# One decoder layer on Trainium2: the MLP's two products as seven products of half-size blocks, in two stages with the combinations of u in DRAM

## The chip, the cores and the metric

The kernel runs on one core of a Trainium2 chip. The time is device microseconds of one execution; for the kernel before it is the median of 3 runs, 2079.65 us (2079.5 to 2080.16). Five engines of the core appear in the profile: PE (TensorE, the matrix products), DVE (VectorE), ACT (ScalarE), POOL (GpSimd) and SP, whose queue issues all the large DMA transfers here. PSUM is the memory that PE adds up into, in banks of 128 x 512 fp32; SBUF holds tiles of 128 partitions; DRAM is the chip's HBM.

## The reference, cut to what matters

One layer of a decoder with three mixers side by side, all in fp32; sequence 1024, width 1024, MLP width 4096.

```python
for l in range(DEPTH):                      # DEPTH = 1
    h = rms_norm(x, norm_mix_g[l])
    z_a, z_bx, z_by, z_q, z_k, z_v, z_g = split_cols(h @ w_in[l], IN_SIZES)
    ...                                     # three mixers, their projections, their gates
    merged = gates[:, :, 0] * y_a + gates[:, :, 1] * y_b + gates[:, :, 2] * y_c
    x = x + merged @ w_out[l]                        # 1024 x 1024 x 1024
    u = rms_norm(x, norm_mlp_g[l]) @ mlp_up[l]       # 1024 x 1024 x 4096
    x = x + jnp.square(jax.nn.relu(u)) @ mlp_down[l] # 1024 x 4096 x 1024
```

The change touches the last three lines alone.

## The kernel before

Every fp32 product of a 128 x 128 block with 512 columns is made of three matmuls: each operand is split in a rounded part "hi" and the rest "lo", and `mm3` adds hi·hi, hi·lo and lo·hi into one PSUM bank. `load_w` brings 512 KB of a weight from DRAM, casts hi on ACT (L225) and makes lo on POOL as raw − hi (L226); its rings hold 2 raw and 3 split blocks. PSUM has 8 banks, drawn from rings with the tags "g", "s" and "w" of two banks each and two single ones, "ac0" and "ac1".

`tail` is the end of the layer. It has these parts.

- **w_out.** For 4 groups of 256 columns two weight blocks are loaded, and for each of the 8 row tiles one bank takes 24 matmuls of 256 columns; DVE adds it to x2, which stays in SBUF (L1273). With the last column group each row tile is normalised (`norm_tile`, L254 to L256) into xn.
- **norm_split.** xn is transposed on PE, four 128 x 128 blocks to a bank (L264); ACT writes the scaled hi into hh (L266), DVE the lo into hl (L267). hh and hl hold the transposed, normalised x in two halves of 512 rows of the sequence. The first half is done among the w_out matmuls, the second half (`second_half`) after them.
- **up(f)**, 32 times. A block of 128 columns of mlp_up against both halves: 2 banks of 24 matmuls each. `ev` takes u out of the bank: relu and its square as hi on ACT (L1301, L1302), the square again on DVE in fp32 (L1303), lo on POOL (L1304). u stays in SBUF, in rings of 4.
- **down(c)**, 16 times, after the up blocks of the next chunk. Two 128-row blocks of mlp_down are loaded and split (ACT L1316, POOL L1317), and for each of 8 row tiles and 2 column halves a bank takes 6 matmuls; DVE adds each bank to x2 (L1325). With the last chunk each row tile is stored to the output (L1327).

The order of instructions on each engine is not written out by hand. The program is written in the order of the loops, and the framework's scheduler places each engine's instructions at build time by its own model of when they are ready; the semaphores then follow from the tiles that are read and written. A tile whose ring is full waits for the last reader of the tile that it replaces.

Of the kernel before, what the change touches and what calls it, by code (L numbers as in the profile page):

```python
# [18 lines left out]
P = 128  # L19
# [105 lines left out]
def hybrid_block(ctx, tc, io, out, dbg=None):  # L125
# [103 lines left out]
    def mm3(ps, pairs, first=True, last=True):  # L229

        n = len(pairs)
        for i, (lh, ll, rh, rl) in enumerate(pairs):
            PE.matmul(ps, lh, rh, start=first and i == 0, stop=False)  # L233
            PE.matmul(ps, lh, rl, start=False, stop=False)  # L234
            PE.matmul(ps, ll, rh, start=False, stop=last and i == n - 1)  # L235
# [1016 lines left out]
def tail(tc, io, last, dbg, psum, pg, mh_pool, mhi, mlo, load_w, mm3, gemm_pieces, norm_tile, norm_split, out):  # L1252
    nc = tc.nc
    V, A, G, S = nc.vector, nc.scalar, nc.gpsimd, nc.sync
    x2d, outd = io["x"][0], out[0]
    with tc.tile_pool(name="x2", bufs=1) as xp:
        x2 = xp.tile([P, 8, D], F32, name="x2")
        with tc.issue_after(last.ins):
            for i in range(8):
                S.dma_start(x2[:, i, :], x2d[i * P : (i + 1) * P, :])  # L1260
        hh, hl = ([xp.tile([P, KT, H], F32R, name=f"{nm}0")] for nm in ("hh2", "hl2"))
        n2 = tc.tile_pool(name="n2", bufs=2)
        np2 = n2.__enter__()
        xns = {}
        for n in range(4):
            cs = slice(n * 256, n * 256 + 256)
            wt = [load_w(io["w_out"][0][512 * q : 512 * q + 512, cs].rearrange("(k p) c -> p k c", p=P), [P, 4, 256], f"wo{n}{q}")
                  for q in range(2)]
            for i in range(8):
                ps = psum("s", 2, f"wo{n}{i}") if i % 2 else pg.tile([P, 512], F32, tag="g", name=f"wo{n}{i}")  # L1270
                hf, ts_ = i // 4, slice(i % 4 * P, (i % 4 + 1) * P)
# [10 lines left out]
        with tc.tile_pool(name="h2", bufs=1, side="right") as h2:  # L1282
# [8 lines left out]
            with tc.tile_pool(name="wd", bufs=1) as wd, tc.tile_pool(name="mu", bufs=2) as mu:  # L1291
# [38 lines left out]
                for c in range(nchunk + 1):  # L1330
# [3 lines left out]
                    if c > 0:  # L1334
                        down(c - 1)
# [24 lines left out]
```

## Time and profile before

| | |
|---|---|
| time, median of 3 runs | 2079.65 us (2079.5 to 2080.16) |
| time of the profiled execution | 2078.28 us |
| its span, first to last instruction | 2076.5 us |
| mean granted TensorE clock | 0.988 |
| all before w_out | about 1265 us of the span |
| w_out with the first half of the norm | about 1265 to 1360 us |
| second half of the norm, first up blocks | about 1360 to 1400 us |
| up and down blocks in turn | to 2072 us |
| w_out matmuls of 256 columns | 768 |
| MLP matmuls of 512 columns | 3072 |

The busy times of the profile are sums over instructions of an engine; PE and PEld are matmuls and the weight loads that run beside them. Matmuls overlap in the records: each of 512 columns shows about 390 ns, but they follow one another more closely, so the time of a stage is read from how many of them fall into a window and not from their durations. "idle before, releaser" gives what ended an engine's idle time. PEclk is the clock that PE was granted, 1.0 being full speed.

### The profile page before, as it was taken

What the parts mean: (1) busy time and instruction counts of PE and PEld (TensorE: products, weight loads), DVE (VectorE), ACT (ScalarE), POOL (GpSimd) and SP (SyncE); (2) the same over time, 40 slices, a digit from 0 to 9 for tenths busy, and PEclk for the clock granted to TensorE, in tenths of its full rate; (3) what the DMA queues carried; (4) which work ended last, traced back from release to release, by engine and by line L of the source; (5) the groups of instructions that cost most, each with busy time, mean ns of one, the idle gap of its engine ahead of it and who ended that gap; (6) DMA issues with size and microseconds to landing.
All of it is one profiled execution on the core that took longest, in us unless ns stands there. A gap on an engine that the chain in (4) does not pass through costs nothing. (4 is left out here: it accounts for less than half of the span.)

```text
span 2076.5 us, 30629 instructions
## 1 busy us (share of the span) xinstructions
PE 2012.3 (97%) x12486; PEld 1616.5 (78%) x12486; DVE 954.5 (46%) x1830; ACT 632.1 (30%) x1117; POOL 667.4 (32%) x606
## 2 busy tenths in 40 slices
PE   6999999999999999999999999999999999999999
PEld 4766777787778778677777789978888888888887
DVE  5665456556656653332342443163344443434434
ACT  5665223323332322332333222152221122211210
POOL 2223442344243331211543422135332233322320
PEclk9999999999999999999999999999999999999999
DMA  4222311222122214432543334122111111111102
GB/s 140 58 68 72 90 54 46 55 74 57 48 53 68 55 53 150 127 114 92 168 123 100 117 105 148 52 62 81 51 51 41 41 53 59 44 49 41 39 13 82
DMA packets 191907, 155.32 MB, mean 75 GB/s; under 512 B 36264, under 2 KB 167493, under 8 KB 191766
## 3 DMA queue, kind: packets, MB, share of 16 engines
q1 hardware_dynamic: 191590, 153.34, 24.6%
q8 instruction: 98, 1.61, 0.3%
q14 instruction: 43, 0.35, 0.1%
q0 software_dynamic: 160, 0.02, 0.0%
q10 hardware_dynamic: 16, 0.00, 0.0%
HBM read 125.15 MB, written 30.55 MB: 75 GB/s over the span
## 5 line engine op out<-in xcount | busy, mean ns | idle before, releaser
L1325 DVE TENSOR_TENSOR x<-dn,x 128x512 f32<-128x512 f32 x256 | 174.6, 689 | 256.4 <-PE dn L235 256.2
L233 PE MATMUL g_up<-hh,wh_up 128*128 128x512 f32 x512 | 199.8, 391 | 1.4 <-ACT r L1301 1.4
L234 PE MATMUL g_up<-hl,wh_up 128*128 128x512 f32 x512 | 200.7, 392 | 0.2 <-DVE hl L267 0.2
L235 PE MATMUL g_up<-hh,wl_up 128*128 128x512 f32 x512 | 199.6, 390 | 0.0
L233 PE MATMUL dn<-dh,uh 128*128 128x512 f32 x512 | 199.2, 389 | 0.0
L234 PE MATMUL dn<-dl,uh 128*128 128x512 f32 x512 | 199.2, 389 | 0.0
L235 PE MATMUL dn<-dh,ul 128*128 128x512 f32 x512 | 199.2, 389 | 0.0
L1303 DVE TENSOR_TENSOR r<-r 128x512 f32<-128x512 f32 x64 | 106.3, 1662 | 147.9 <-ACT uh L1302 147.9
L1317 POOL TENSOR_TENSOR dl<-dr,dh 128x1024 fp32r<-128x1024 f32 x32 | 76.7, 2419 | 285.0 <-ACT dh L1316 285.0
L233 PE MATMUL g_zg<-hh,wh_zg 128*128 128x512 f32 x384 | 155.5, 405 | 0.0
L234 PE MATMUL g_zg<-hl,wh_zg 128*128 128x512 f32 x384 | 152.8, 398 | 0.0
L235 PE MATMUL g_zg<-hh,wl_zg 128*128 128x512 f32 x384 | 152.6, 397 | 0.0
L1316 ACT CAST dh<-dr 128x1024 fp32r<-128x1024 f32 x32 | 32.3, 1052 | 318.0 <-PE dn L235 314.3
L233 PEld LDWEIGHTS g_up<-hh,wh_up 128*128 128x128 f32 x512 | 96.3, 188 | 21.8 <-ACT r L1301 1.9
L234 PEld LDWEIGHTS g_up<-hl,wh_up 128*128 128x128 f32 x512 | 96.3, 188 | 20.0 <-DVE hl L267 0.7
L234 PEld LDWEIGHTS dn<-dl,uh 128*128 128x128 f32 x512 | 96.2, 188 | 20.0
L235 PEld LDWEIGHTS dn<-dh,ul 128*128 128x128 f32 x512 | 96.1, 188 | 19.9
L233 PEld LDWEIGHTS dn<-dh,uh 128*128 128x128 f32 x512 | 96.1, 188 | 19.8
L235 PEld LDWEIGHTS g_up<-hh,wl_up 128*128 128x128 f32 x512 | 96.3, 188 | 19.4
L1304 POOL TENSOR_TENSOR ul<-r,uh 128x512 fp32r<-128x512 f32 x64 | 83.8, 1310 | 85.3 <-DVE r L1303 85.3
L226 POOL TENSOR_TENSOR wl_zg<-wr_zg,wh_zg 128x1024 fp32r<-128x1024 f32 x24 | 58.7, 2448 | 163.1 <-ACT wh_zg L225 145.3
L226 POOL TENSOR_TENSOR wl_up<-wr_up,wh_up 128x1024 fp32r<-128x1024 f32 x32 | 76.8, 2401 | 84.8 <-ACT wh_up L225 44.4
(435 smaller groups left out, 4622.8 us busy)
## 6 DMA issues: line engine op xcount, KB each, us to landing
wr_up<-in_mlp_up_dram SPq DMA_DIRECT2D x32, 512.0 KB
dr<-in_mlp_down_dram SPq DMA_DIRECT2D x32, 512.0 KB
wr_zg<-in_w_in_dram SPq DMA_DIRECT2D x24, 512.0 KB
mg_d<-th SPq DMA_DIRECT2D x32, 256.0 KB
tb<-mg_d SPq DMA_DIRECT2D x32, 256.0 KB
wr_z<-in_w_in_dram SPq DMA_DIRECT2D x12, 512.0 KB
qk_d<-zo SPq DMA_DIRECT2D x24, 256.0 KB
z<-qk_d SPq DMA_DIRECT2D x12, 512.0 KB
```

What stands on the lines that cost most here:

```text
L226: G.tensor_tensor(lo, raw, hi, ALU.subtract)
L233: PE.matmul(ps, lh, rh, start=first and i == 0, stop=False)
L234: PE.matmul(ps, lh, rl, start=False, stop=False)
L235: PE.matmul(ps, ll, rh, start=False, stop=last and i == n - 1)
L1303: V.tensor_tensor(r, r, r, ALU.mult)
L1304: G.tensor_tensor(ul[:, sl], r, uh[:, sl], ALU.subtract)
L1316: A.copy(h, raw)
L1317: G.tensor_tensor(l, raw, h, ALU.subtract)
L1325: V.tensor_tensor(x2[:, i, sl], ps, x2[:, i, sl], ALU.add)
```

## The change

`tail` is written anew. The MLP's up and down products are each made by a scheme of 2 x 2 blocks with seven block products in place of eight (Strassen, in Winograd's form with shared sums).

- **Up.** The transposed, normalised x is B with blocks B11 (first 512 of the model's width, first 512 rows of the sequence), B21, B12 and B22. Four combinations T1, T2, T3, T4 are made of them once and kept split, beside B11, B21 and B22. For each of 8 groups g of 512 columns of mlp_up the weights' four blocks are combined on DVE (L1402, L1403, L1414, L1419) and split (`wsplit`: ACT L1342, POOL or DVE L1343). Seven products of 24 matmuls follow. X and Y are pairs of PSUM banks, and products are added up in them in place: a copy out (L1377, L1408, L1413) takes the state of the bank between two products. DVE adds (L1390, L1418, L1425) give the four blocks of u; `relu2` is relu and square in one operation (L1395).
- **u in DRAM.** The four blocks and three sums of u that the down product needs (seven in all) are written as 512 KB each to the DRAM tensor u_d, for every group. They leave from three SBUF tiles, "l4", "l5" and "r1", which every group uses again. "l4" holds c11 (in the code also a11) and a12.
- **Down.** After all of the up product, 4 rounds kg of 1024 of the MLP's rows each: seven products of 48 matmuls; each loads one of the seven u combinations of two groups, splits it (ACT, DVE L1343) and splits a combination of mlp_down's blocks (ACT, POOL). Four banks X and four Y are added up in place as before, and `out_add` (L1513) adds them to the accumulators, which were loaded again from x2_d in DRAM.
- **w_out.** For each half of the sequence and each half of the columns four banks are filled over four weight loads, with 512 columns a matmul (384 of them). x2 is stored to DRAM (L1338). `second_half(j)` transposes column block j of both halves of the width (L1306) and makes B22, T1, T2 and T3 from them; `first_half` makes B11 and B21.

The removed lines are those of `tail` printed above. The added ones, cut:

```diff
+                for q in range(4):
+                    wh, wl = load_w(io["w_out"][0][256 * q : 256 * q + 256, half[n]].rearrange("(k p) c -> p k c", p=P), [P, 2, H], f"wo{hf}{n}{q}")
+                    for i in range(4):
+                        ts_ = slice(i * P, (i + 1) * P)
+                        mm3(pss[i], [(mhi[2 * q + k][hf][:, ts_], mlo[2 * q + k][hf][:, ts_], wh[:, k, :], wl[:, k, :]) for k in range(2)],
+                            first=q == 0, last=q == 3)
+                    if hf == 1 and n == 0 and q > 0:
+                        first_half(range(3 * q - 3, min(3 * q, 8)))
+                for i in range(4):
+                    t = 4 * hf + i
+                    V.tensor_tensor(x2[t][:, half[n]], pss[i], x2[t][:, half[n]], ALU.add)
+                    if n == 1:
+                        norm_tile(t)
+                        S.dma_start(x2_d[t], x2[t])
+        def split(src, hi, lo, E):
+            A.copy(hi, src)
+            E.tensor_tensor(lo, src, hi, ALU.subtract)
+            return hi, lo
...
+        def up_a(g):
+            X = st[g]["X"] = [psum(f"ac{m}", 1, f"ux{g}{m}") if g % 2 else psum("s", 2, f"ux{g}{m}") for m in range(2)]
+            w = wsplit(st[g][0][:, :, 0:256], G, f"a11{g}")
+            for m in range(2):
+                up_product(g, w, "B11", X, True, (m,))
+                yield
+            def outputs():
+                uo = [blk(t, [P, 2, 2, H], f"uo{g}{t}") for t in ("l4", "l5", "r1")]
+                st[g]["u"] = [uo[i // 2][:, i % 2] for i in range(6)]
+                for m in range(2):
+                    A.copy(st[g]["u"][0][:, m, :], X[m])
+            if g > 1:
+                outputs()
+            w = wsplit(st[g][1][:, :, 0:256], G, f"a12{g}")
+            Y = [pg.tile([P, 512], F32, tag="g", name=f"uy{g}{m}") for m in range(2)]
+            for m in range(2):
+                up_product(g, w, "B21", Y, True, (m,))
+                yield
+            if g < 2:
+                outputs()
+            c11 = st[g]["u"][0]
+            for m in range(2):
+                V.tensor_tensor(c11[:, m, :], Y[m], c11[:, m, :], ALU.add)
+            relu2(c11)
+            S.dma_start(u_d[g, 0], c11)
+        def relu2(c):
+            V.scalar_tensor_tensor(c, c, 0.0, c, ALU.max, ALU.mult)
+        def up_b(g):
+            r0, r1, X = st[g][0], st[g][1], st[g]["X"]
+            a11, a12, a21, a22, s1, s2 = st[g]["u"]
+            w11, w21, w12, w22 = r0[:, :, 0:256], r0[:, :, 256:512], r1[:, :, 0:256], r1[:, :, 256:512]
+            t1, t2 = wtmp(f"s1{g}"), wtmp(f"s2{g}")
+            V.tensor_tensor(t1, w21, w22, ALU.add)
+            V.tensor_tensor(t2, t1, w11, ALU.subtract)
+            w = wsplit(t2, G, f"s2{g}")
+            up_product(g, w, "T2", X, False)
+            u1 = sm2.tile([P, 2, H], F32, tag="u1", name=f"u1{g}")
+            for m in range(2):
+                A.copy(u1[:, m, :], X[m])
+            w = wsplit(t1, V, f"s1{g}")
+            Y = [pg.tile([P, 512], F32, tag="g", name=f"uz{g}{m}") for m in range(2)]
+            up_product(g, w, "T1", Y, True)
+            for m in range(2):
+                A.copy(a22[:, m, :], Y[m])
+            V.tensor_tensor(w21, w21, w11, ALU.subtract)
+            w = wsplit(w21, G, f"s3{g}")
+            up_product(g, w, "T3", X, False)
+            for m in range(2):
+                V.tensor_tensor(a22[:, m, :], X[m], a22[:, m, :], ALU.add)
+            V.tensor_tensor(w12, w12, t2, ALU.subtract)
+            w = wsplit(w12, G, f"s4{g}")
+            up_product(g, w, "B22", Y, False)
+            relu2(a22)
+            S.dma_start(u_d[g, 3], a22)
+            for m in range(2):
+                V.tensor_tensor(a21[:, m, :], Y[m], u1[:, m, :], ALU.add)
+            w = wsplit(w22, V, f"a22{g}")
+            up_product(g, w, "T4", X, False)
+            relu2(a21)
+            V.tensor_tensor(s1, a21, a22, ALU.add)
+            S.dma_start(u_d[g, 4], s1)
+            V.tensor_tensor(s2, s1, a11, ALU.subtract)
+            S.dma_start(u_d[g, 5], s2)
+            V.tensor_tensor(a21, a21, a11, ALU.subtract)
+            S.dma_start(u_d[g, 6], a21)
+            for m in range(2):
+                A.activation(a12[:, m, :], X[m], AF.Relu)
+            V.tensor_tensor(a12, a12, a12, ALU.mult)
+            S.dma_start(u_d[g, 1], a12)
+            V.tensor_tensor(a22, a12, s2, ALU.subtract)
+            S.dma_start(u_d[g, 2], a22)
...
+        def second_half(j):
+            p12, p22 = transposed(1, j), transposed(1, 4 + j)
+            g0, g1 = pc("mg", j), pc("mg", 4 + j)
+            t = blk(f"l{4 + j % 2}", [P, 4, H], f"tt{j}")
+            b22, t1, t2, t3 = (t[:, i, :] for i in range(4))
+            h, l = B["B22"]
+            A.activation(b22, p22, AF.Copy, scale=g1)
+            V.scalar_tensor_tensor(t1, p12, g0, b11[:, j, :], ALU.mult, ALU.subtract)
+            V.scalar_tensor_tensor(t2, p22, g1, t1, ALU.mult, ALU.subtract)
+            A.activation(h[:, j, :], p22, AF.Copy, scale=g1)
+            V.scalar_tensor_tensor(t3, p12, g0, b22, ALU.mult, ALU.subtract)
+            V.scalar_tensor_tensor(l[:, j, :], p22, g1, h[:, j, :], ALU.mult, ALU.subtract)
+            for nm, x, E in (("T2", t2, G), ("T1", t1, V), ("T3", t3, G)):
+                split(x, B[nm][0][:, j, :], B[nm][1][:, j, :], E)
+            V.tensor_tensor(b21[:, j, :], b21[:, j, :], t2, ALU.subtract)
...
+        next(steps[0])
+        next(steps[0])
+        second_half(0)
+        next(steps[0])
+        second_half(1)
+        next(steps[0])
+        second_half(2)
+        next(steps[1])
+        second_half(3)
+        next(steps[1])
...
+        for g in range(8):
+            for _ in steps[g]:
+                pass
+            up_b(g)
+            if g + 2 < 8:
+                up_raw(g + 2)
...
+            def product(i, w, bk, start):
+                raw = u_raw(kg, i)
+                for c in range(2):
+                    uh, ul = u_split(raw, kg, i, c)
+                    wh, wl = wsplit(w[c], G, f"d{kg}{i}{c}")
+                    for t in range(4):
+                        ts_ = slice(t * P, (t + 1) * P)
+                        mm3(bk[t], [(uh[:, m, ts_], ul[:, m, ts_], wh[:, m, :], wl[:, m, :]) for m in range(2)],
+                            first=start and c == 0, last=c == 1, skip=True)
+            X = banks(True, f"dx{kg}")
+            product(0, b11_, X, True)
+            Y = banks(False, f"dy{kg}")
+            product(1, b21_, Y, True)
+            for t in range(4):
+                out_add(kg, X[t], t, 0)
+            for c in range(2):
+                V.tensor_tensor(t1[c], b12_[c], b11_[c], ALU.subtract)
+                V.tensor_tensor(t2[c], b22_[c], t1[c], ALU.subtract)
+            product(5, t2, X, False)
+            for t in range(4):
+                out_add(kg, Y[t], t, 0)
+                store(kg, t, 0)
+            Y = banks(False, f"dz{kg}")
+            product(4, t1, Y, True)
+            for t in range(4):
+                out_add(kg, X[t], t, 1)
+            for c in range(2):
+                V.tensor_tensor(b12_[c], b12_[c], b22_[c], ALU.subtract)
+            product(6, b12_, X, False)
+            for t in range(4):
+                out_add(kg, Y[t], 4 + t, 1)
+            product(2, b22_, Y, False)
+            for t in range(4):
+                out_add(kg, X[t], 4 + t, 1)
+                store(kg, 4 + t, 1)
+            for c in range(2):
+                V.tensor_tensor(b21_[c], b21_[c], t2[c], ALU.subtract)
+            product(3, b21_, X, False)
+            for t in range(4):
+                out_add(kg, Y[t], t, 1)
+                store(kg, t, 1)
+            for t in range(4):
+                out_add(kg, X[t], 4 + t, 0)
+                store(kg, 4 + t, 0)
```

u_d's second index is the number of the combination: 0 is c11, 1 is a12, 3 is a22, 4 and 5 are the sums s1 and s2, 2 and 6 two differences.

How it stands on three engines, in the program's order (the names are tiles; g, k and bank numbers are in them, and the last number is the tile's own).

PE at the joint between the norm and the up stage, before. nt_f0 and nt_f1 are transposes of the first and second half of the sequence, g_up0 the first block of the up product:

```order
L264 MATMUL nt_f07_12524<-cg_92,xn_f3_12337 128x128
L234 MATMUL g_up0_0_12650<-hl20_11512,wh_up0_12646 128x512
L235 MATMUL g_up0_0_12650<-hh20_11511,wl_up0_12647 128x512
L233 MATMUL g_up0_0_12650<-hh20_11511,wh_up0_12646 128x512
L264 MATMUL nt_f10_12579<-cg_92,xn_f4_12378 128x128
L264 MATMUL nt_f10_12579<-cg_92,xn_f5_12419 128x128
L264 MATMUL nt_f10_12579<-cg_92,xn_f6_12488 128x128
L264 MATMUL nt_f10_12579<-cg_92,xn_f7_12557 128x128
L234 MATMUL g_up0_0_12650<-hl20_11512,wh_up0_12646 128x512
L235 MATMUL g_up0_0_12650<-hh20_11511,wl_up0_12647 128x512
L233 MATMUL g_up0_0_12650<-hh20_11511,wh_up0_12646 128x512
```

Up matmuls of the first half stand between the transposes of the second. After (ux11 is the last bank of the products that need the first half alone, ux00 with T2 the first product that needs T2):

```order
L234 MATMUL ux11_12350<-B11l_11818,wh_a111_12351 128x512
L235 MATMUL ux11_12350<-B11h_11817,wl_a111_12352 128x512
L1306 MATMUL nt_f15_12294<-cg_92,xn2_11499 128x128 x2
L1306 MATMUL nt_f15_12294<-cg_92,xn3_11500 128x128 x2
L1306 MATMUL nt_f12_12325<-cg_92,xn2_11499 128x128 x2
L1306 MATMUL nt_f12_12325<-cg_92,xn3_11500 128x128 x2
L1306 MATMUL nt_f16_12330<-cg_92,xn2_11499 128x128 x2
L1306 MATMUL nt_f16_12330<-cg_92,xn3_11500 128x128 x2
L1306 MATMUL nt_f13_12367<-cg_92,xn2_11499 128x128 x2
L1306 MATMUL nt_f13_12367<-cg_92,xn3_11500 128x128 x2
L1306 MATMUL nt_f17_12372<-cg_92,xn2_11499 128x128 x2
L233 MATMUL ux00_12217<-T2h_12207,wh_s20_12432 128x512
```

The last transposes now follow one another with no product between them, and the next thing on PE is the product with T2, which needs all of them.

DVE between two PSUM sums in the steady part, before (dn are banks of the down product, r is u before its split):

```order
L1325 TENSOR_TENSOR x2_11502<-dn171_13322,x2_11502 128x512
L1303 TENSOR_TENSOR r60_13363<-r60_13363 128x512
L1303 TENSOR_TENSOR r61_13393<-r61_13393 128x512
L1303 TENSOR_TENSOR r70_13431<-r70_13431 128x512
L1325 TENSOR_TENSOR x2_11502<-dn200_13478,x2_11502 128x512
L1303 TENSOR_TENSOR r71_13461<-r71_13461 128x512
```

and after, at the end of group 2 (uz2 are the two Y banks after the sixth product, uo2l4, uo2l5 and uo2r1 the three tiles that are stored, ur31 a raw weight block of group 3):

```order
L1425 TENSOR_TENSOR uo2l5_12850<-uz20_12927,u12_12920 128x512
L1425 TENSOR_TENSOR uo2l5_12850<-uz21_12928,u12_12920 128x512
L1395 SCALAR_TENSOR_TENSOR uo2l5_12850<-uo2l5_12850 128x1024
L1429 TENSOR_TENSOR uo2r1_12851<-uo2l5_12850 128x1024
L1419 TENSOR_TENSOR ur31_12817<-ur31_12817,s23_13134 128x4x256
L1431 TENSOR_TENSOR uo2r1_12851<-uo2r1_12851,uo2l4_12849 128x1024
L1433 TENSOR_TENSOR uo2l5_12850<-uo2l5_12850,uo2l4_12849 128x1024
L1437 TENSOR_TENSOR uo2l4_12849<-uo2l4_12849 128x1024
L1439 TENSOR_TENSOR uo2l5_12850<-uo2l4_12849,uo2r1_12851 128x1024
```

Where two adds and four short squares stood, a row of operations of 128 x 1024 stands, each on the result of the one before or on the same tile, and a12 (L1437) is the last but one.

ACT at the start of group 4, before:

```order
L1301 ACTIVATE r60_13363<-g_up6_0_13338 128x512
L1302 ACTIVATE uh6_13330<-r60_13363 128x512
L225 CAST wh_up9_13678<-wr_up9_13676 128x1024
L1301 ACTIVATE r61_13393<-g_up6_1_13368 128x512
L1302 ACTIVATE uh6_13330<-r61_13393 128x512
```

and after (L1436 is the relu of group 3's a12, L1377 the copy of group 4's first product to c11, in the tile "l4" that a12 of group 3 leaves):

```order
L1436 ACTIVATE uo3l4_13094<-ux30_13064 128x512
L1342 CAST wh_s24_13382<-s24_13379 128x1024
L1436 ACTIVATE uo3l4_13094<-ux31_13065 128x512
L1342 CAST wh_s14_13413<-s14_13378 128x1024
L1377 COPY uo4l4_13339<-ux40_13309 128x512
L1377 COPY uo4l4_13339<-ux41_13310 128x512
L1342 CAST wh_s34_13446<-ur40_13060 128x1024
L1408 COPY u14_13410<-ux40_13309 128x512
```

Two evacuations and a cast per bank have become a chain in which the copy to c11 stands behind the last casts of two weight combinations and ahead of the next cast.

More of the change, by code (lines that the diff above doesn't have):

```diff
@@ L227, in load_w, with mm3 @@
         return hi, lo
-    def mm3(ps, pairs, first=True, last=True):
+    def mm3(ps, pairs, first=True, last=True, skip=False):
         n = len(pairs)
         for i, (lh, ll, rh, rl) in enumerate(pairs):
-            PE.matmul(ps, lh, rh, start=first and i == 0, stop=False)
-            PE.matmul(ps, lh, rl, start=False, stop=False)
-            PE.matmul(ps, ll, rh, start=False, stop=last and i == n - 1)
+            PE.matmul(ps, lh, rh, start=first and i == 0, stop=False, skip_group_check=skip)
+            PE.matmul(ps, lh, rl, start=False, stop=False, skip_group_check=skip)
+            PE.matmul(ps, ll, rh, start=False, stop=last and i == n - 1, skip_group_check=skip)
     def load_cols(w2d, c0, n, nm):
@@ L361, in hybrid_block @@
     mhp = mp.__enter__()
-    mhi, mlo = ([[mhp.tile([P, H], F32R, name=f"{nm}{k}{hf}") for hf in range(2)] for k in range(KT)] for nm in ("mhi", "mlo"))
+    mt = {(x, hf, q): mhp.tile([P, 4, H], F32R, tag=f"r{4 * hf + 2 * x + q}", name=f"m{'hl'[x]}{hf}{q}")
+          for hf in range(2) for x in range(2) for q in range(2)}
     mhp.tile([P, 248], F32, name="pad1")
+    mhi, mlo = ([[mt[(x, hf, k // 4)][:, k % 4, :] for hf in range(2)] for k in range(KT)] for x in range(2))
     last = gates_c(tc, io, psum, gt, zs, ths, mhi, mlo, yc, load_pc, pws[0], mm3)
@@ L366, in hybrid_block @@
     hpool.__exit__(None, None, None)
-    tail(tc, io, last, dbg, psum, pg, mp, mhi, mlo, load_w, mm3, gemm_pieces, norm_tile, norm_split, out)
+    tail(tc, io, last, psum, pg, wp, mhp, mhi, mlo, load_w, mm3, tiny_rsqrt, pc, ident, out)
+    mp.__exit__(None, None, None)
 def attn_values(tc, io, hh, hl, load_w, mm3, pg, wp, v_d):
@@ L1249, in gates_c, with tail @@
     return last
[L1252 removed]
+def tail(tc, io, last, psum, pg, wp, rp, mhi, mlo, load_w, mm3, tiny_rsqrt, pc, ident, out):
     nc = tc.nc
[L1254 removed]
+    V, A, G, S, PE = nc.vector, nc.scalar, nc.gpsimd, nc.sync, nc.tensor
     x2d, outd = io["x"][0], out[0]
[L1256 to L1335 removed]
```

171 lines of the change are left out of this document (119 added, 52 removed).

## The prediction

> **What bounds the kernel now.** I read the page from the top: busy time, slices, chain of waits; then a table by stage, since the change touches only the last third of the span.
>
> ```profile
> span 2076.5 us, 30629 instructions
> PE 2012.3 (97%) x12486; PEld 1616.5 (78%) x12486; DVE 954.5 (46%) x1830; ACT 632.1 (30%) x1117; POOL 667.4 (32%) x606
> PE   6999999999999999999999999999999999999999
> PE 42%; DVE 1%; DMA 0%; SPq 0%; ACT 0%; issue 0%; DVEq 0%; ACTq 0%
> ```
>
> TensorE (PE) is busy in every slice, and of the chain it holds 42% against 1% for the next engine. The stages, by hand-set borders (us of the span; columns: PE, PEld, VectorE (DVE), ScalarE (ACT), GpSimd (POOL) busy, granted clock, DMA share, GB/s):
>
> ```profile
> 1265.00:1372.00 107.00, 104.23 (x831) 101.85 (x830) 40.38 (x106) 26.89 (x45) 21.42 (x9) 0.99 0.27 90
> 1372.00:1380.00 8.00, 8.00 (x42) 6.59 (x41) 4.48 (x7) 4.07 (x7) 0.71 (x1) 0.92 0.00 0
> 1380.00:1400.00 20.00, 18.40 (x90) 14.54 (x90) 7.25 (x7) 10.06 (x14) 8.52 (x5) 1.00 0.33 106
> 1400.00:2070.00 670.00, 670.00 (x2958) 554.96 (x2957) 273.89 (x315) 130.01 (x178) 220.42 (x121) 1.00 0.16 48
> 1286.00:1340.00 54.00, 54.00 (x452) 54.00 (x451) 8.07 (x19) 6.30 (x6) 11.14 (x5) 1.00 0.13 40
> ```
>
> The MLP runs from 1400 to 2070 with no PE gap at full clock: 670 / 2958 = 0.2265 us for one 512-column matmul. No engine beside PE is over half busy there (DVE 274 of 670). So the time of this stage is the count of matmuls. In the last row, inside w_out, 54.00 / 452 = 0.1195 us pass per 256-column matmul, and the weight-load column is full too.
>
> **What the change takes away.** The up product has 32 blocks of 48 matmuls, the down product 16 chunks of 96: 3072. After it there are 8 groups of 7 products of 24, and 4 of 7 products of 48: 2688. 384 fewer × 0.2265 = −87.0 us. w_out goes from 768 matmuls of 256 columns (768 × 0.1195 = 91.8) to 384 of 512 (384 × 0.2265 = 87.0): −4.8 us. Its 16 loads are cast and split in 16 × (1.05 + 2.41) us of ACT and POOL (L1316, L1317 below), side by side under 87 us of PE, so I cost them at nothing. The sum holds only where PE still waits for nothing, so the rest of the sum is a search for waits.
>
> **What it adds in the up stage.** Prices first. A DVE add that reads PSUM, and the 128x1024 operations from SBUF:
>
> ```profile
> L1325 DVE TENSOR_TENSOR x<-dn,x x256: 673/692/692, 1420.8 to 2072.2; 128x512 f32<-128x512 f32 x128
> L932 DVE SCALAR_TENSOR_TENSOR gwa<-gwa,th x4: 1212/1224/1226, 80.8 to 161.9; 128x1024 f32<-128x1024 f32 x4
> L1317 POOL TENSOR_TENSOR dl<-dr,dh x32: 2397/2406/2854, 1393.8 to 2013.2; 128x1024 fp32r<-128x1024 f32 x32
> L1316 ACT CAST dh<-dr x32: 1043/1050/1056, 1392.2 to 2010.6; 128x1024 fp32r<-128x1024 f32 x32
> ```
>
> (min/median/max ns). A group lasts 168 × 0.2265 = 38.05 us of PE, a product 5.44. In it DVE has 14 operations of 1.22 and 6 adds of 0.69: 21.2 us; POOL 5 lo parts of 2.41: 12.0; ACT 7 casts of 1.05 and 8 copies or relus of about 0.6: 12.2. The queue moves seven 512 KB stores of u and 2 MB of weights, 5.7 MB in 38 us or 150 GB/s, against
>
> ```profile
> HBM read 125.15 MB, written 30.55 MB: 75 GB/s over the span
> 1276.00:1280.00 4.00, 4.00 (x35) 4.00 (x34) 1.88 (x4) 0.09 (x1) 0.00 (x0) 1.00 1.03 418
> ```
>
> 418 GB/s at its best. All of this fits, also with DVE and POOL held to one at a time (33.2 of 38.05). That they hold one another up is seen here:
>
> ```profile
> L1303 DVE TENSOR_TENSOR r<-r x64: 678/1826/2899, 1378.5 to 2030.7; 128x512 f32<-128x512 f32 x64
> 1510.91 1.30 POOL L1304 TENSOR_TENSOR ul<-r,uh 128x512 fp32r<-128x512 f32 x1 [0.63 <-DVE r L1303]
> 1509.01 1.82 DVE L1303 TENSOR_TENSOR r<-r 128x512 f32<-128x512 f32 x1 [0.49 <-ACT uh L1302]
> 1507.88 2.40 POOL L226 TENSOR_TENSOR wl_up<-wr_up,wh_up 128x1024 fp32r<-128x1024 f32 x1 [3.37 <-PE dn L235]
> ```
>
> The square L1303 reads SBUF twice and takes 0.678 us at its fastest, 1.826 in the median: in the third and fourth lines it starts while POOL is busy and ends 0.55 us after POOL does. L1325, of the same size but with one input in PSUM, never takes over 0.692. The Trainium skill, page "SBUF — State Buffer", section "Who interferes with whom", says the same in stronger words: a DVE operation on two SBUF inputs and a GpSimd access to SBUF exclude each other altogether. The trace agrees.
>
> What counts is the end of each group, where the new operations follow one another. Counted from the end of the sixth product (line L1425 reads its bank): two adds of 0.69, relu² 1.22, s1 1.22, the next group's combination 1.22, s2, a21 − a11 and a12² at 1.22 each, 8.7 us on DVE; two POOL lo parts fall inside and hold it up by 1.5 to 3.5. So a12 is stored 10 to 12.3 us after that product. The store must land before ScalarE may overwrite its tile with the next group's c11 (L1377), and that copy frees the bank in which the next group's second-last accumulation, T2, goes on. The one store of 512 KB whose landing shows:
>
> ```profile
> 2072.23 0.69 DVE L1325 TENSOR_TENSOR x<-dn,x 128x512 f32<-128x512 f32 x1 [0.67 <-PE dn L235]
> ```
>
> ends at 2072.92 and the span, with that tile's store as its last work, at 2076.5: 3.6 us. With a copy of 0.6 the bank is free at 14.2 to 16.5; T2 is due after three products, T4 of this group and two of the next, at 3 × 5.44 = 16.3. The slack is 2.1 to −0.2 us. Bounds: nothing for all 8 groups, or, with the five stores of a group end in the queue ahead of it (five times 3.6 less the 3.6 counted, of which a rate of 418 GB/s would need 6.3 in all), some 4 us × 7 joints = 28. I take 4 us, nearer the low end, since the row at 418 GB/s shows that neighbouring transfers run side by side. The other joints of a group (T1's copy, T3's adds, the lo parts) have 2.6 us or more to spare by the same durations and I cost them at nothing; their cover is one product of PE work, 5.44 us.
>
> **The joint of norm and up stage.** Before, the last transposes are mixed with up matmuls that have no other need of them:
>
> ```profile
> 1365.63 0.63 PE L264 MATMUL nt_f<-cg,xn_f 128*128 128x128 f32 x4 [0.63 <-DVE hl L267]
> 1369.10 0.66 PE L264 MATMUL nt_f<-cg,xn_f 128*128 128x128 f32 x4 [2.14 <-DVE hl L267]
> 1369.00:1371.00 2.00, 1.90 (x10) 1.56 (x10) 1.73 (x7) 0.69 (x1) 0.00 (x0) 0.73 0.78 225
> 1371.00:1373.00 2.00, 2.00 (x8) 1.60 (x8) 1.70 (x4) 0.69 (x1) 0.00 (x0) 0.50 0.01 2
> ```
>
> It loses about 4.3 us there: 0.63 + 2.14 of waits and, after the 2.14, 2 × 0.27 + 2 × 0.50 = 1.5 by the clock of the last two rows. After the change each pair of transposed columns (L1306) holds both banks of its kind until six DVE and ACT operations have read them, with seven more operations behind:
>
> ```profile
> L267 DVE SCALAR_TENSOR_TENSOR hl<-nt_f,par,hh x16: 739/751/752, 1359.0 to 1388.9; 128x512 fp32r<-128x512 f32 x16
> L1302 ACT ACTIVATE uh<-r x64: 622/632/637, 1377.7 to 2029.4; 128x512 fp32r<-128x512 f32 x64
> L1304 POOL TENSOR_TENSOR ul<-r,uh x64: 1282/1288/1755, 1379.3 to 2031.4; 128x512 fp32r<-128x512 f32 x64
> ```
>
> Per pair DVE has four scaled subtractions of 0.75, a lo part and an update of 0.68 or more, ACT five of 0.63 to 0.69, POOL two of 1.29. The next pair's transposes wait for the reads. Four pairs on DVE, with POOL's holds, take about 4 × 6 = 24 us, and with the copies of c11 queued on ACT behind the last casts T2 cannot start before about 32 us after the first pair. PE has 68 matmuls (15.4 us) and the transposes (32 × 0.14 = 4.5) to fill that: about 12 us idle, and by the rows above 3 us more lost to the clock. Less the old 4.3: +10.7, and with T4's lo parts in front of the first group +12. Bounds: +5, if POOL's holds fall beside ACT's work, and +22, if PE idles through all of the 24 us and keeps half the clock for what follows.
>
> **The down stage.** u comes back from DRAM and is split again. One of 4 rounds is 336 × 0.2265 = 76.1 us of PE. DVE has 14 lo parts and 8 combinations of 1.22 and 28 adds of 0.69: 46.2 us; POOL 14 lo parts: 33.7; ACT 28 casts: 29.4; the queue 11.3 MB, 149 GB/s. Before there are 256 adds for this, now 112. Even by turns DVE and POOL need 79.9 of 76.1 only if no PSUM add lies beside POOL, which L1325 shows that it may; less these 19.3 it is 60.6. The first round needs u of the last groups and 4 MB of accumulators from DRAM (10 us at 418 GB/s, begun under the last up group): boundary 0 to 8 us, rounds 0 to 12 together. I take 6 for both. The end stays as it is: two adds and a store after the last product, before and after.
>
> **Sum.** −87.0 − 4.8 + 12 + 4 + 6 = −69.8 us. The profiled execution, 2078.28 us, would become 2008.5; the median of the runs shown, 2079.65, is 1.4 above it, so 2010 us, 3.4% faster.
>
> **Rivals.**
> - *The store chain binds.* If a12 lands 2 to 4 us late at each of 7 joints, it adds 14 to 28 us, and each such wait is as long as the 2.14 us after which the clock fell to 0.50; at half clock over 3 us another 1.5 to 2 per joint, 10 to 14 together. Time 2030 to 2048 (against the 4 us taken). For it: the slack of about nothing. Against it: 150 GB/s wanted, 418 shown. The page "TensorE: Matmul & The Clock Gate" of the Trainium skill, Part 1, gives an idle window of about 3.4 us for the fall to half clock; by that rule waits of 2 us would cost themselves alone, and the row with 0.50 after 2.14 us speaks for the dearer case.
> - *DVE and POOL by turns bind the down stage.* 4 × (79.9 − 76.1) = 15 us, 2025. For it: L1303's median of 1.826. Against: half of DVE's work reads PSUM.
> - *Hidden better than I think.* The joints cost nothing and the transition 5: 2079.65 − 91.8 + 5 = 1993.
> - *Slower than before.* One mechanism: the queue of stores at the group ends. If five stores of 512 KB drain one after the other at 3.6 us each, a12 lands 18 us after its issue instead of 3.6, 14 late in each of 7 joints: 100 us, 30 more than the gain of 70, about 2108. It decides from 70 / 7 = 10 us a joint. Against it: 512 KB in 3.6 us is 146 GB/s, a third of what the 1276 row shows for transfers together.
> - *It saves no PE time.* If something other than the count set 1400 to 2070, the time would stay at 2080 with the joints added; the full PE column excludes nearly all of this.
>
> **How the numbers follow.** Main case 0.62 (2000 to 2022), hidden better 0.10, store chain 0.13, DVE with POOL 0.09, no gain 0.02, slower 0.04. The range reaches from 1994 to 2046. Faster (by over 0.2%, about 4 us, which is what a measurement of this kernel can tell) 0.94, same 0.02, slower 0.04.
>
> **What would show it.** Right: PE matmuls of 512 columns still 0.2265 apart inside the up groups and down rounds, about 695.8 − 608.8 less of it; one gap of about 12 us before the first T2, released by c11's ACT copy; gaps under 1 us at the later T2s; L1425 to the a12 store in 10 to 12 us. Wrong: gaps at each T2 released by a DMA (first rival); DVE over 0.9 busy in the down stage with PE waiting for u's lo parts (second); granted clock under 0.9 over more than the transition.

## The result, and the profile after

The changed kernel takes 2015.01 us (median of 4, 2011.14 to 2019.47), the kernel before 2079.57 (median of 4, 2072.32 to 2080.16): ratio 0.9698, interval 0.9665 to 0.9731. In a second comparison it took 2010.10 (2007.67 to 2013.76) against 2075.61: 0.9685 (0.9665 to 0.9706). 2010 was forecast. The profiled execution took 2018.17 us with a span of 2016.4, which is 60.1 less than before.

The page of the changed kernel:

```profile
span 2016.4 us, 29583 instructions
PE 1928.2 (96%) x11718; PEld 1528.2 (76%) x11718; DVE 1146.4 (57%) x1872; ACT 717.3 (36%) x1189; POOL 732.8 (36%) x592
PE   6999999999999999899999999997899999999999
PE 35%; DVE 4%; issue 1%; DMA 1%; ACT 0%; POOL 0%; SPq 0%; DVEq 0%; ACTq 0%; POOLq 0%
```

PE is still the bound: 84.1 us less of it, and 60.1 of span. Three slices show 8, 7 and 8 where all had been 9; the first of them, at 807 to 857 us, lies ahead of w_out and so ahead of the change. DVE has 4% of the chain. What is to be read is where the gaps of the other two lie. The stages of the changed kernel (columns as before; first row w_out and norm up to the first matmul with T2, then group 0, group 1, the groups 2 to 6 and 7 up to its T2, the rest of 7, the first down round with the start of the second, the other rounds, the end):

```profile
1271.40:1404.60 133.20, 118.01 (x533) 96.20 (x531) 65.49 (x118) 55.55 (x86) 56.77 (x27) 0.95 0.42 151
1404.60:1433.86 29.26, 29.24 (x121) 24.02 (x122) 20.65 (x21) 9.68 (x15) 14.01 (x6) 0.93 0.24 88
1433.86:1474.96 41.10, 34.70 (x145) 28.26 (x144) 23.49 (x21) 10.60 (x15) 11.45 (x4) 0.92 0.38 141
1474.96:1676.90 201.94, 201.44 (x889) 166.48 (x887) 137.86 (x107) 61.52 (x80) 80.95 (x26) 1.00 0.43 158
1676.90:1704.30 27.40, 27.36 (x121) 22.66 (x122) 16.87 (x15) 12.28 (x16) 12.23 (x4) 1.00 1.01 389
1704.30:1790.50 86.20, 83.51 (x366) 68.17 (x365) 82.63 (x63) 29.43 (x30) 40.20 (x15) 1.00 0.59 220
1790.50:2012.30 221.80, 221.80 (x981) 183.64 (x979) 170.66 (x138) 77.14 (x77) 99.76 (x39) 1.00 0.32 116
2012.30:2016.40 4.10, 0.38 (x2) 0.00 (x0) 0.69 (x1) 0.00 (x0) 0.00 (x0) 0.99 0.33 128
```

Row four is five groups on end and a part of the last, without a wait but for 0.5 us (889 matmuls at 0.227), row seven almost three down rounds without any. The time that did not come off lies in rows one, three and six. The PE rows at the longer gaps of rows one to four, with what ended them:

```profile
1353.11 0.50 PE L233 MATMUL wo<-wh_wo,mh 128*128 128x512 f32 x1 [1.85 <-ACT b L1315]
1382.95 0.50 PE L233 MATMUL ux<-B11h,wh_a 128*128 128x512 f32 x1 [2.52 <-ACT wh_a L1342]
1393.33 0.63 PE L1306 MATMUL nt_f<-cg,xn 128*128 128x128 f32 x4 [2.60 <-DVE tt L1456]
1395.80 1.08 PE L1306 MATMUL nt_f<-cg,xn 128*128 128x128 f32 x4 [1.84 <-DVE B22l L1457]
1399.36 1.09 PE L1306 MATMUL nt_f<-cg,xn 128*128 128x128 f32 x4 [2.47 <-DVE tt L1456]
1404.62 0.79 PE L233 MATMUL ux<-T2h,wh_s 128*128 128x512 f32 x1 [2.92 <-ACT uo0l L1377]
1445.86 0.79 PE L233 MATMUL ux<-T2h,wh_s 128*128 128x512 f32 x1 [6.40 <-ACT uo1l L1377]
1676.94 0.50 PE L233 MATMUL ux<-T2h,wh_s 128*128 128x512 f32 x1 [0.53 <-ACT uo7l L1377]
```

Both matmuls of 0.79 are at half clock (0.39 is their usual time): the granted clock was low in a stretch that begins before each of these two waits ends and outlasts it:

```profile
1395.20:1408.60 13.40, 7.24 (x21) 5.28 (x22) 11.83 (x16) 9.07 (x16) 9.86 (x8) 0.50 0.49 158
1443.00:1449.50 6.50, 3.64 (x9) 2.87 (x10) 4.65 (x5) 1.07 (x2) 0.00 (x0) 0.50 0.55 175
```

Single runs of one kernel lie up to 14 us apart, and the instructions ahead of w_out are the same in both kernels. So the kernels are compared below by the stretch from the first w_out matmul to the end of the span: 809.9 us before (from 1266.6), 745.0 after (from 1271.4), which is −64.9.

### The profile page after: what moved, and what is told of

The parts are those of the page before. It is cut to its first block, busy times and chain, and to the rows that moved or that the text cites. A ratio compares the mean times of both kernels' runs of the same rounds, so it can differ in the third digit from the quotient of the medians.

```text
span 2016.4 us, 29583 instructions
## 1 busy us (share of the span) xinstructions
PE 1928.2 (96%) x11718; PEld 1528.2 (76%) x11718; DVE 1146.4 (57%) x1872; ACT 717.3 (36%) x1189; POOL 732.8 (36%) x592
## 5 line engine op out<-in xcount | busy, mean ns | idle before, releaser
L1343 POOL TENSOR_TENSOR wl_d<-dr,wh_d 128x1024 fp32r<-128x1024 f32 x40 | 102.6, 2564 | 129.1 <-ACT wh_d L1342 129.1
L1343 DVE TENSOR_TENSOR du<-dq,du 128x1024 fp32r<-128x1024 f32 x56 | 125.5, 2240 | 21.6 <-ACT du L1342 21.0
L235 PE MATMUL dx<-wh_d,du 128*128 128x512 f32 x256 | 99.8, 390 | 2.7 <-DVE du L1343 2.7
L234 PE MATMUL dx<-wl_d,du 128*128 128x512 f32 x256 | 99.6, 389 | 0.0
L233 PE MATMUL dx<-wh_d,du 128*128 128x512 f32 x256 | 99.6, 389 | 0.0
L1342 ACT CAST wh_d<-dr 128x1024 fp32r<-128x1024 f32 x40 | 42.1, 1052 | 144.8 <-PE dx L235 79.0
L233 PEld LDWEIGHTS g_zg<-hh,wh_zg 128*128 128x128 f32 x384 | 72.8, 190 | 18.1 <-issue 3.6
L235 PEld LDWEIGHTS g_zg<-hh,wl_zg 128*128 128x128 f32 x384 | 72.5, 189 | 16.3 <-issue 1.5
L234 PEld LDWEIGHTS g_zg<-hl,wh_zg 128*128 128x128 f32 x384 | 72.8, 190 | 15.7 <-issue 1.8
L1343 POOL TENSOR_TENSOR wl_a<-ur,wh_a 128x1024 fp32r<-128x1024 f32 x16 | 51.0, 3188 | 83.9 <-ACT wh_a L1342 83.9
L234 PE MATMUL g_z<-hl,wh_z 128*128 128x512 f32 x192 | 77.6, 404 | 0.0
L235 PE MATMUL g_z<-hh,wl_z 128*128 128x512 f32 x192 | 77.2, 402 | 0.0
L233 PE MATMUL g_z<-hh,wh_z 128*128 128x512 f32 x192 | 76.7, 400 | 0.4 <-DVE zsq L420 0.4
L1343 POOL TENSOR_TENSOR wl_s<-ur,wh_s 128x1024 fp32r<-128x1024 f32 x16 | 42.6, 2662 | 82.9 <-ACT wh_s L1342 82.9
```

Source lines behind the costliest of these rows:

```text
L233: PE.matmul(ps, lh, rh, start=first and i == 0, stop=False, skip_group_check=skip)
L234: PE.matmul(ps, lh, rl, start=False, stop=False, skip_group_check=skip)
L235: PE.matmul(ps, ll, rh, start=False, stop=last and i == n - 1, skip_group_check=skip)
L1342: A.copy(hi, src)
L1343: E.tensor_tensor(lo, src, hi, ALU.subtract)
```

## The experiments

**The measure itself.** The changed kernel run again.

> The changed kernel once more. Theory (the 7 us between single runs of one kernel lie ahead of the changed code, whose w_out starts between 1260.8 and 1272.2 us in the six profiles so far): from the first w_out matmul to the end 744 to 746 us again, wherever w_out starts. Rival (the spread lies in the MLP's waits): over 2 us from 745.0.

```profile
0.00:1262.50 1262.50, 1206.45 (x8571) 936.22 (x8572) 629.33 (x1396) 461.41 (x875) 418.76 (x473) 0.99 0.30 87
1262.50:2006.70 744.20, 716.11 (x3149) 589.35 (x3147) 518.38 (x477) 256.46 (x314) 315.41 (x120) 0.98 0.43 156
```

w_out starts 8.9 us earlier than in the first profile, and the stretch after it is 744.2, 0.8 less than 745.0 (0.3 of it in the wait at the last group, 0.21 in place of 0.53). The spread lies ahead of the change, and differences of 2 us in the stretch can be read, though every other kernel was profiled only once. 4.8 of the difference between −64.9 and −60.1 is thereby not the change's.

**What a matmul is worth.** Up stage and down stage with eight products:

> An eighth product in the up stage (the second product is made twice) and in the down stage (the first is made twice); the numbers that come out are no longer the layer's. It has as many MLP matmuls as the kernel before, 3072, in the new structure. Theory (PE bound, each matmul 0.2267): 384 x 0.2267 = 87.1 us more than the changed kernel, less 5 to 8 at the joint of groups 0 and 1, which gets a product of cover more: about 2094, or 12 to 20 us over the kernel before. Rival (the seven products do not shorten what binds, the added DVE, POOL and DMA work does): under 60 us more than the changed kernel.

```diff
                 up_product(g, w, "B21", Y, True, (m,))
+                up_product(g, w, "B21", Y, False, (m,))
...
+                    if i == 0:
+                        for t in range(4):
+                            ts_ = slice(t * P, (t + 1) * P)
+                            mm3(bk[t], [(uh[:, m, ts_], ul[:, m, ts_], wh[:, m, :], wl[:, m, :]) for m in range(2)],
+                                first=False, last=c == 1, skip=True)
```

2080.67 us, ratio to the kernel before 1.0015 (0.9998 to 1.0032). The stretch is 812.7: 67.7 more than the changed kernel, 2.8 more than before.

```profile
1260.80:2073.50 812.70, 797.32 (x3533) 658.74 (x3531) 510.84 (x477) 256.19 (x314) 310.94 (x120) 0.99 0.39 143
```

So with 3072 matmuls on PE to hide it, all the new DVE, POOL and DMA work costs 2.8 us net; this kernel also has w_out's 4.8 us of PE work less, so before that saving it is up to 7.6. And 384 matmuls, 87.1 us, are worth 67.7 when taken away: 19.4 come back as waits. In this kernel the waits at the joint of groups 0 and 1 (8.5 with its clock), at the last group (0.7) and in the first down round (3.6) are gone, and the first T2 comes 132.7 us after the first w_out matmul, with 5.4 us more matmuls ahead of it, where it was 133.2: 5.9. Together 18.7. I had expected only 5 to 8 of this, and so about 2094 us in place of 2080.67: the theory stands as a mechanism, its size was missed.

**The joint of groups 0 and 1.** The changed kernel's chain there, on POOL, DVE, SP and ACT:

```profile
1440.44 2.48 POOL L1343 TENSOR_TENSOR wl_s<-ur,wh_s 128x1024 fp32r<-128x1024 f32 x1 [7.62 <-ACT wh_s L1342]
1440.65 3.35 DVE L1403 TENSOR_TENSOR s<-s,ur 128x1024 f32<-128x1024 f32 x1
1440.75 0.32 SPq L1438 DMA_DIRECT2D u_d<-uo0l  x1
1443.93 1.21 DVE L1439 TENSOR_TENSOR uo0l<-uo0l,uo0r 128x1024 f32<-128x1024 f32 x1
1445.22 1.07 ACT L1377 COPY uo1l<-ux 128x512 f32<-128x512 f32 x2 [4.85 <-DVE uo0l L1439]
```

The last matmul of group 0's sixth product starts at 1428.19 and so ends, at 0.227 a matmul, at 1428.42; a12 is stored 12.3 us later, the upper end of the prediction's 10 to 12.3. The copy to c11 then waits for a reader of a12 that I had not counted, the sum L1439, which stands behind a combination that POOL stretches to 3.35 us. In the groups after that it is the store, as forecast:

```profile
1519.86 0.32 SPq L1438 DMA_DIRECT2D u_d<-uo2l  x1
1522.70 1.07 ACT L1377 COPY uo3l<-ux 128x512 f32<-128x512 f32 x2 [3.14 <-DMA u_d<-uo2l]
```

2.8 us from issue to the copy, bank free in time for T2 with some 0.6 us to spare. At the last group the copy comes 4.1 us after the store's issue, and T2 waits 0.53. Two kernels ask why only group 1 waits.

> Only the pairing of tiles is changed: c11 shares its tile with a21 instead of a12, so the copy to c11 of the next group no longer waits for a12's square, its store and the sum a22 that reads it. Theory (the chain of group ends is what costs 8.5 us at the joint of groups 0 and 1, 6.4 of wait and 1.9 of reduced clock, and 0.5 at the last, and nothing at the others): the wait of T2 in group 1 falls from 6.4 to 0 to 2 us, and the time by 6 to 9 us. Rival (that wait is set by group 1's weights or its matmul operands, and the copy only ends last by little): the wait stays above 4 us and the time within 3 us.

```diff
-                st[g]["u"] = [uo[i // 2][:, i % 2] for i in range(6)]
+                st[g]["u"] = [uo[i][:, x] for i, x in ((0, 0), (1, 0), (0, 1), (1, 1), (2, 0), (2, 1))]
```

2003.60 us (0.9642, 0.9618 to 0.9665); the stretch is 735.2, 9.8 less. The wait is 1.27 us:

```profile
1433.28 0.50 PE L233 MATMUL ux<-T2h,wh_s 128*128 128x512 f32 x1 [1.27 <-ACT uo1l L1377]
```

Of the 9.8, 7.2 are this joint (8.5 to 1.3), 0.7 the last group's; the first T2 came 1.6 earlier, which the pairing does not explain.

> The two halves of group 1's first product are no longer made ahead, between the transposes, but in group 1. Theory (this product, 5.44 us, is cover that the transition takes from the joint of groups 0 and 1): the wait for c11 in group 1 falls from 6.4 to 0 to 1.5 us, the idle time before the first T2 grows by 3 to 5.4 us, and the time stays within 4 us of the changed kernel. Rival (the wait at group 1 belongs to the first group end itself, not to the missing product): it stays at 5 us or more and the time rises by 5.

```diff
         second_half(2)
-        next(steps[1])
         second_half(3)
-        next(steps[1])
```

1999.92 us (0.9641, 0.9613 to 0.9670); the stretch is 736.0, 9.0 less, where the theory had the time within 4 us. Group 1's wait is gone, as the theory said. But the transition did not grow for it: the first T2 comes 127.3 us after the first w_out matmul, 6.0 earlier, though only 5.4 us of matmuls had gone.

```profile
1382.61 0.63 PE L1306 MATMUL nt_f<-cg,xn 128*128 128x128 f32 x4 [2.69 <-DVE tt L1456]
1385.76 1.09 PE L1306 MATMUL nt_f<-cg,xn 128*128 128x128 f32 x4 [2.52 <-DVE B22l L1457]
1389.16 1.09 PE L1306 MATMUL nt_f<-cg,xn 128*128 128x128 f32 x4 [2.31 <-DVE tt L1456]
...
1394.17 1.09 PE L1306 MATMUL nt_f<-cg,xn 128*128 128x128 f32 x4 [2.66 <-DVE tt L1456]
...
1399.44 0.80 PE L233 MATMUL ux<-T2h,wh_s 128*128 128x512 f32 x1 [2.92 <-ACT uo0l L1377]
```

These five waits are 13.1 us; those of the changed kernel that take 0.5 us or more, from 1382.95 to the first T2, are 13.2. The product made ahead had covered nothing: it waited 2.5 us itself for its weights and held up the transposes behind it. Half of the theory (that it was the transition's cover) falls; the other half (that it was taken from group 1's joint, which has two products between T4 and T2 in place of three) holds.

**The store chain.** Three more stores ahead of a12:

> s1, s2 and a21 are stored twice (the second time to a tensor that nobody reads), so three more stores of 512 KB stand in the queue ahead of a12 in each group. Theory (transfers run side by side; a12's landing has 0.2 to 0.6 us of slack): a12 lands 0 to 1.5 us later, 0 to 9 us in all over 7 joints. The rival of the prediction (stores drain one after the other at 3.6 us each): a12 lands 8 to 11 us later, 55 to 75 us in all, and slower than 2070.

```diff
             S.dma_start(u_d[g, 4], s1)
+            S.dma_start(v_d[g, 0], s1)
...
```

2023.18 us (0.9730, 0.9698 to 0.9762); the stretch is 751.0, 6.0 more.

```profile
1519.14 0.41 SPq L1442 DMA_DIRECT2D u_d<-uo2l  x1
1523.17 1.07 ACT L1378 COPY uo3l<-ux 128x512 f32<-128x512 f32 x2 [4.33 <-DMA u_d<-uo2l]
```

From issue to copy 4.0 us in place of 2.8: a wait of 0.44 to 0.53 at four of the joints, 1.7 and 2.2 at two. Three more stores cost 1.2 us. The rival in which they drain one by one at 3.6 us each, the one that would have made the kernel slower than before, needed 8 to 11 us a group and is excluded. Whether they run side by side, or one after the other at the full rate, this does not tell: the queue moves 421 GB/s from this issue to this copy, which is 1.2 us for each 512 KB.

**w_out alone.**

> The kernel before with one part of the change alone: w_out in four passes of four banks with 512 columns a matmul, 16 loads in place of 8; norm and MLP as they were. Counted from the first w_out matmul to the end of the span, which is 809.9 us in the kernel before. Theory (the sum's term: 768 x 0.1195 against 384 x 0.2265): 4 to 6 us less by the matmuls, and 0 to 5 more because the last four row tiles are all normalised after the last w_out matmul instead of one by one: 804 to 810. Rival (the norm is what the changed kernel's transition waits for): 5 us longer or more, 815 and over.

2075.14 us against 2075.61 (0.9991, 0.9978 to 1.0004); the stretch is 808.0, 1.9 less.

```profile
1364.40 0.44 PE L264 MATMUL nt_f<-cg,xn_f 128*128 128x128 f32 x2 [2.32 <-DVE xn_f L256]
1365.83 0.69 PE L264 MATMUL nt_f<-cg,xn_f 128*128 128x128 f32 x2 [0.99 <-DVE xn_f L256]
```

The 4.8 us of the matmul count turn for the larger part into waits for the last row tiles' norm, in which four now come at once, and into the half clock behind them (6.8 us at 0.50, where the kernel before has 3.4).

**The transition.** Its order (below, from `second_half` of column block j; T1, T3 and b21 follow in a second pass over j):

> The changed kernel with group 1's first product not made ahead, as before, and the second half of the norm made in another order: t1 and t2 of each column block go to tiles of their own (l3 and l5), only t1, t2, B22 and T2 are made between the transposes, T1, T3 (now as b11 - t2, the same in exact arithmetic) and the update of b21 after them; c11's tile l4 is no longer used as a temporary. From the first w_out matmul to the end the changed kernel takes 745.0 us and the one without the product ahead 736.0. Theory (the transition costs 13 us of PE waits because each pair of transposes waits for operations that T2 doesn't need and c11's copy for its tile): 5 to 10 us of these waits go, 726 to 731. Rival (DVE and POOL together are full in the transition whatever the order): 734 to 738.

```diff
-            A.activation(b22, p22, AF.Copy, scale=g1)
             V.scalar_tensor_tensor(t1, p12, g0, b11[:, j, :], ALU.mult, ALU.subtract)
             V.scalar_tensor_tensor(t2, p22, g1, t1, ALU.mult, ALU.subtract)
             A.activation(h[:, j, :], p22, AF.Copy, scale=g1)
-            V.scalar_tensor_tensor(t3, p12, g0, b22, ALU.mult, ALU.subtract)
             V.scalar_tensor_tensor(l[:, j, :], p22, g1, h[:, j, :], ALU.mult, ALU.subtract)
...
+            split(t2, B["T2"][0][:, j, :], B["T2"][1][:, j, :], G)
```

1998.47 us (0.9630, 0.9605 to 0.9656); the stretch is 730.7: 5.3 less than without the product ahead, near the theory's worse end. T2 now starts 113.6 us after the first w_out matmul, 13.7 earlier, among the transposes. The longest waits that stay are one ahead of it and one behind it:

```profile
1378.78 1.11 PE L1306 MATMUL nt_f<-cg,xn 128*128 128x128 f32 x4 [2.29 <-DVE tt L1455]
1396.80 0.50 PE L234 MATMUL ux<-T2l,wh_s 128*128 128x512 f32 x1 [2.75 <-POOL T2l L1343]
```

So c11's tile and the operations of no use to T2 were, together, a real barrier, and once they are gone the lo parts on POOL are the next. The waits from the transposes to the end of group 0 fall from 13.4 to 6.8 us.

> The kernel of the new order with c11 paired with a21 as well. Theory: the wait of 0.5 us at the last group joint goes and nothing else, 0 to 1.5 us less than the new order alone. Rival (pairing gained its 9.8 us elsewhere than at the joint of groups 0 and 1, so it adds up): 3 us or more less.

1996.94 us (0.9611, 0.9586 to 0.9635); the stretch is 728.8, 1.9 less: the last group's wait, 1.54 us in the kernel of the new order, is gone. The two edits do not add up, so the larger part of the pairing's gain was the joint of groups 0 and 1.

**DVE and POOL by turns.**

> The kernel with both edits (new order of the norm, c11 paired with a21), with one more: in the down stage DVE makes the lo parts of the weights in place of POOL. From the first w_out matmul to the end the kernel with both edits takes 728.8 us. By the rows a round then has DVE 46.2 + 14 x 1.22 = 63.3 us of 76.1 and nothing of POOL. Theory (the 3.6 us of the first down round come from POOL and DVE holding one another up: DVE's lo parts there take up to 3.4 us in place of 1.22): the waits for u's lo parts in the first round fall to under 1 us in all, 725 to 727. Rival (DVE has too much of its own in the first round, the sums left over from the up stage and the combinations of two rounds, so that 17 us more make it later): 729 to 740.

```diff
-                    wh, wl = wsplit(w[c], G, f"d{kg}{i}{c}")
+                    wh, wl = wsplit(w[c], V, f"d{kg}{i}{c}")
```

1994.31 us (0.9603, 0.9582 to 0.9623); the stretch is 725.0, 3.8 less. (The intervals of the two ratios overlap; it is the stretch that shows the difference.) The lo parts of u, first in the changed kernel, then here, and the whole down stage, first with both edits alone, then here:

```profile
L1343 DVE TENSOR_TENSOR du<-dq,du x56: 1206/2577/3411, 1686.3 to 1993.1; 128x1024 fp32r<-128x1024 f32 x56
```

```profile
L1343 DVE TENSOR_TENSOR du<-dq,du x56: 1214/1218/1226, 1668.8 to 1971.1; 128x1024 fp32r<-128x1024 f32 x56
```

```profile
1685.50:1993.90 308.40, 305.32 (x1344) 251.91 (x1343) 253.79 (x200) 106.78 (x107) 141.21 (x54) 1.00 0.40 149
```

```profile
1685.80:1990.20 304.40, 304.40 (x1344) 252.06 (x1343) 232.44 (x253) 107.11 (x107) 0.00 (x0) 1.00 0.41 149
```

DVE does 53 operations more in this stage and is busy 21 us less, since none is stretched any more; POOL does nothing, and PE has no gap. This is the strongest form of the sharing that L1303 had shown before the change.

> As the kernel with DVE's lo parts in the down stage, and in the up stage too: there DVE has 21.2 + 5 x 1.22 = 27.3 us of 38.05 per group. Theory (POOL's 2.4 us shut DVE out, so 1.22 on DVE itself is cheaper even for DVE): the operations from the sixth product's end to a12's square end at 10 to 12 us instead of 12.2, no new waits, within 2 us of the one with the down stage alone. Rival (lo parts wait behind the chain of sums in DVE's order, so that a product waits for its weights at each group end): 1 to 3 us for each of 8 groups, 8 to 24 us more.

1994.55 us (0.9603, 0.9578 to 0.9627); the stretch is 725.2. a12's square ends 10.1 us after the sixth product in place of 12.2 (group 0 keeps 12.3), and c11's copy waits for a store only once, 1.1 us; PE waited for neither in the kernel it is built on, so no time comes of it. One new wait of 1.1 us for a lo part stands in group 0, where none was forecast. These two are the fastest versions by the stretch, 0.8 to 1.0% under the changed kernel by their ratios.

## Why the prediction was right, point by point

By its own terms, in the stretch, the sum −69.8 against −64.9:

- **Matmuls, −87.0.** Right as PE work: 0.227 us each in row four and in the down rounds. As time they are worth 67.7; the prediction had the missing 19.4 in its other terms, as 12 + 4 + 6 of stalls.
- **w_out, −4.8.** By itself it gave 1.9, so 2.9 came back in the next term: the saved matmuls uncovered the norm, where I had named only the casts and lo parts as work to hide. The changed kernel loses more inside w_out, which the prediction put at nothing: the last pass takes two of its banks from the ring of the transposes and waits 1.85 us until ACT has read the last of these (L1315, first of the PE rows at the gaps), and the half clock behind it costs some 1.6. The kernel with the new w_out alone uses the same ring without this wait; there two operations read each transposed bank, here three.
- **The transition, +12.** The first row's stretch has 111.9 us of PE work by the rows (384 and 72 and 12 matmuls of 0.2267, 64 transposes that follow one another by 0.09) and takes 133.2, and the first T2 product 2.0 more than its matmuls: 23.3 lost. By the same count the kernel before loses 8.5 in all, where the prediction had read 4.3, so +14.8, with the norm behind w_out and w_out's own wait in it. The waits were forecast at 12 and are 13.4; the clock was forecast at 3 and cost some 4: of the 13.7 us at 0.50, PE stands in waits for 6.3, and half of the other 7.4 is lost. In place of one gap released by c11's copy there are six of over 0.5 us, and that copy ends only the last, of 2.92. The chain named (each pair of transposes waits for the readers of its banks, then c11's copy) is the one in the trace for 9.8 of the 13.2 us; the other 3.4 are the weights of the product made ahead, which the prediction did not name. The new order showed that this chain, not the amount of DVE work, set about half of the waits.
- **Group joints, +4.** 9.2 us: 8.5 in group 1 (6.4 of wait, 1.9 of clock, the rest in the matmul behind the wait), 0.7 in group 7 (0.53 of wait), nothing in the others. The slack at the steady joints, 0.6 us (12.2 us to the store, 2.8 to land in place of 3.6, 16.3 due), lies inside the forecast 2.1 to −0.2. The step that failed is "after three products": the order of PE, which stands in the text on the change, has group 1's first product ahead of the last transposes, so its joint has two. The reader L1439 was left out as well.
- **Down stage, +6.** 3.6, all in the first round, by DVE and POOL holding one another up, the second rival's mechanism in a place where it had not been put; over the other rounds there is no wait. The exclusion that the prediction cites from the Trainium skill, page "SBUF — State Buffer", section "Who interferes with whom", is stated there for a GpSimd instruction that reads SBUF and not for one that only writes it; POOL's lo parts read two tiles.
- **The end, 0.** −0.6 (4.1 us from the last matmul in place of 4.7).

−87.0 − 4.8 + 14.8 + 9.2 + 3.6 − 0.6 is −64.8, 0.1 from the measured −64.9. The forecast's closeness is in part luck: the transition and the joints came out 8.0 worse than forecast, the down stage and the end 3.0 better. One of the prediction's signs of being wrong showed at one place, the clock at 0.50 for 6.8 us in group 1, and "gaps under 1 us at the later T2s" failed there alone. The rivals: the store chain binds at no steady joint; DVE and POOL cost 3.6 of 15; the serial queue is excluded by the doubled stores.

## What to carry to other kernels

When work is taken from the engine that bounds, ask of each piece what it was covering: here 384 matmuls of 87 us gave 68, since 19 us of the other engines' chains came into the open at four joints. Count the cover at every joint from the order of the instructions, not from one typical round: the single joint that was one product short cost 8.5 us, where 4 had been forecast for all seven. And before an engine is called a helper, see what it does to its neighbour: taking POOL out of the down stage made DVE's larger load the shorter one.

## What the runs showed of the hardware

The granted clock is at half in stretches of 3.4 us and multiples of it (3.4, 6.8, 13.7 and 20.5 in the clock's records after w_out's start). The changes lie on a fixed grid: in the changed kernel the clock falls at 1354.10, 1395.06 and 1442.85, which are 12 and 14 steps of 3.413 us apart. The price of a wait is not fixed by its length. At the first matmul of group 1's product ahead, PE waited 2.45 us in the paired kernel and 2.52 in the changed one; the windows of the wait and of what follows, first the paired kernel:

```profile
1373.40:1375.90 2.50, 0.05 (x1) 0.00 (x0) 2.40 (x4) 1.64 (x3) 0.00 (x0) 1.00 0.31 116
1376.90:1380.20 3.30, 2.95 (x9) 2.14 (x8) 2.15 (x2) 3.30 (x6) 3.30 (x2) 0.50 0.00 0
```

```profile
1380.50:1383.00 2.50, 0.05 (x1) 0.06 (x1) 2.38 (x4) 1.57 (x3) 0.03 (x1) 1.00 0.23 88
1383.00:1387.50 4.50, 3.65 (x17) 2.86 (x18) 2.89 (x3) 4.45 (x7) 4.50 (x2) 1.00 0.00 0
```

0.50 after the shorter, 1.00 after the longer. The grid explains it: in the paired kernel 2.42 of the 2.45 us fall into the one step that ends at 1376.89, while in the changed kernel a grid line at 1381.41 splits the 2.52 us into 0.98 and 1.54. Over the steps at full clock in the twelve profiles, from w_out's start on and with waits of over 0.1 us summed, all 16 steps with 1.91 us of waits or more were followed by half clock, none with 1.53 or less, and 6 of 14 between these. The Trainium skill, page "TensorE: Matmul & The Clock Gate", Part 1, has free-running windows of 3413 ns, with which the lengths and the grid agree and which make the price a matter of where in a window the wait falls. That a whole idle window of some 3.4 us is needed for the fall, the runs don't bear out.

The spread between single runs has the same source in good part: ahead of w_out the clock's records are at half for 47.8 us in the profile where w_out starts at 1271.4 and for 34.1 in the one where it starts at 1260.8, which at half speed is 6.9 of the 10.6 us. PE's waits of over 0.15 us there, 58.7 us in the one and 55.7 in the other, give 3.0 more. The clock alone does not set it: with the same 47.8 us, w_out starts at 1266.0 in the paired kernel, where these waits are 56.0. Why waits and clock differ there from run to run stays open.
